# Queries and keys of all head pairs by Strassen's scheme ahead of attention, and the gates' token sums read back from DRAM, in a one-core hybrid trunk kernel

## The chip, the cores and the metric

The kernel runs on one core of a Trainium2 chip. The metric is the device time of one execution in microseconds (us), the median of several runs. The core has a matrix engine (TensorE, PE in the profile, with PEld for its weight loads), a vector engine (VectorE, DVE), an activation engine (ScalarE, ACT), a general engine (GpSimd, POOL), and SyncE (SP), which here only issues DMAs. PE writes its sums into PSUM banks (128 partitions by 512 float32), and DVE and ACT read them from there.

## The reference

One layer of a streaming encoder over 1024 tokens of width 1024, in float32. Cut to what matters:

```python
proj = x @ w_in
q_a, k_a, v_a, f_a, q_b, f_b, i_b, g_b, gate_a, gate_b = split(proj)
# branch A: forgetting attention, 8 heads of 64
F = cumsum(log_sigmoid(f_a + b_f))
y_a = softmax(where(causal, q_a @ k_a.T / 8 + F[t] - F[s], -inf)) @ v_a
# branch B: gated linear recurrence (HGRN2), 4 heads of 128
f = lb + (1 - lb) * sigmoid(f_b)
S_t = diag(f_t) S_{t-1} + (1 - f_t) v_t^T ;  o_t = S_t^T silu(q_b)_t
y_b = rmsnorm(o_b) * norm_g * sigmoid(g_b)
# merge, output projection, layer norm, SwiGLU, layer norm
merged = sigmoid(gate_a) * (y_a @ w_pa) + sigmoid(gate_b) * (y_b @ w_pb)
x = layer_norm(ALPHA * x + merged @ w_o)
x = layer_norm(ALPHA * x + (silu(g) * u) @ w_ff_out)     # u, g = split(x @ w_ff_in)
```

## The kernel before

**Products.** Every large float32 operand is split into a rounded high part and the rest (`split`: a cast on ACT, a subtraction on DVE), and a product is three matmuls, high by high, high by low and low by high (`mm3`, L449). x is held transposed and split in four tiles, `xh` and `xl`, in quarters A11, A12, A21, A22 (token half, and half of the channels).

**Strassen.** Most of the large products go by Strassen's scheme in Winograd's form: seven products p1 to p7 of blocks in place of eight. On the token side they need the quarters themselves (p1, p2, p4) and four sums of quarters: S1 for p5, S2 for p6, S3 for p7, S4 for p3 (`vops`, made for the values from L640 on). On the weight side they need block differences, made on DVE. Results are put together from p1, u2 = p1 + p6, u3 = u2 + p7 and so on. `skip_group_check` with `start=False` lets a product add onto what a bank holds already.

**Stages, in program order.** Values of both branches by Strassen (`vx`, `vy`: all eight banks); forget gates; queries and keys of head pair 0 by Strassen (`qk_first`, L720), while S1 stands in the place of A21, which is then restored from the raw quarter `a21`; attention for pairs 0 to 3 (`attention`, L763), with q and k of the next pair made directly after each (`qk_project`, L708: eight chunks by three matmuls for each of two weights and two token halves, PE's `qps` and `kps`); the recurrence's projections (`hgrn_project`, PE's `bps`) and heads (`hgrn`, L884); gates (`gate`: PE's `gps`; `gate_part`: `ge`; the rest in Strassen pairs, `gs`); branch projections (`pps`); output projection (`o`); layer norm; feed-forward by Strassen (`fa` to `fd`, then `p`); layer norm and output.

**Attention.** For a head, two rows of `box1` hold the broadcast sums of log f, plain and masked; DVE makes the masked row from the plain one and the constant `causal` (L770 to L773). For each block of 128 queries, scores go to a bank, DVE adds the row and takes the running minimum (`tensor_tensor_reduce`), ACT takes the exponential with its sum, DVE the reciprocal, POOL scales the block, PE transposes it, ACT and DVE split it, PE multiplies it with the values. `qk_heads` (L695) turns a bank with q or k of a pair into the tiles q2, k2, kl of its two heads, with the high part in one half of the partitions and the low part in the other.

**Gates.** The last twelve gate blocks go by Strassen. Their token sums S1 to S4 are made anew: x is loaded raw (`xr`, L1129) and `sums4` (L479) subtracts and splits on DVE and ACT.

**Order and storage.** Nothing is issued as it is written down. Each call is put in a list (`Plan.add`), with what it depends on. `Plan.schedule` (L170) places all calls with estimated durations, `improve` (L334) tries several ranks, and `issue` sends them in the best order found; so nearly every instruction of the profile has the line L363. An engine then works its calls strictly in that order. Tiles come from tags with a fixed number of buffers (`BUFS`, L378), handed out in order within a tag, PSUM banks likewise (`SPREAD`). `plan.early` lowers a call's rank, so that the gates' and projections' weights are drawn forward.

```python
    qk = qk_first()
    for p in range(4):
        attention(p, qk)
        if p < 3:
            qk = qk_project(p + 1)
        else:
            qfg = hgrn_project(0)
```

Of the kernel before, what the change touches and what calls it, by code (L numbers as in the profile page):

```python
# [16 lines left out]
P = 128  # L17
# [17 lines left out]
ROUNDS = 20  # L35
MARGIN = 1.06
SLACK = 400.0
SWITCH = 300.0
ALPHA = 2.0 ** 0.25
# [16 lines left out]

class Plan:
# [4 lines left out]
    OWN = {"PE": 0.0, "ACT": 0.0, "DVE": 127.0, "POOL": 60.0, "SP": 2500.0}  # L62
    SETS = {AF.Exp: 0, AF.Ln: 0, AF.Sigmoid: 1, AF.Silu: 2}

    def __init__(self, tc):
        self.tc = tc
        self.calls, self.tiles, self.log, self.first = [], {}, {}, {}
        self.queues, self.rank = {}, []
        self.early = 0
        self.loose = set()  # L70

# [22 lines left out]
    def add(self, q, method, args, kw):  # L94
# [7 lines left out]
        if method == "copy_predicated":  # L102
            ins.append(outs[0])
        n = len(self.calls)
        self.rank.append(n - self.early)
        pred = set()
# [21 lines left out]
        both = sum(str(v.space).endswith("SB") and v.free_size() > 128 for v in ins) > 1  # L128
        self.calls.append((q, method, args, kw, pred, names, fresh, self.cost(q.name, method, outs, ins, kw), both))

    def cost(self, eng, method, outs, ins, kw):
# [27 lines left out]
        if eng == "POOL":  # L159
            if method == "tensor_tensor" and kw.get("op") == ALU.pow:  # L160
# [9 lines left out]
    def schedule(self, slack, wait):  # L170
# [13 lines left out]
        dma_free = 0.0  # L184
        fifo, slots = {}, {}
# [15 lines left out]
        while done < len(calls):  # L201
            best = None
            for q, av in avail.items():
                for i in av:
# [16 lines left out]
                    if not ok:  # L221
                        continue
                    if q == "ACT":
# [14 lines left out]
            if q == "SP":  # L238
                start = max(t + 100, dma_free)
                dma_free = start + d  # L240
                free[q] = t + 60
                fin = dma_free
            else:
# [6 lines left out]
                fin = t + d  # L250
                free[q] = fin
# [35 lines left out]
    def lag(self, i, u, slack):  # L287
        q, uq = self.calls[i][0].name, self.calls[u][0].name
        lat = self.OWN[q] if uq == q else self.LAT[q]
# [4 lines left out]
    def latest(self, slack):  # L294
# [7 lines left out]
        for old, i in self.after:  # L302
            for m in by.get(old, ()):
                users[m].append((i, self.LAT[calls[m][0].name] + 60))
# [29 lines left out]
    def improve(self, slack, wait):  # L334
# [4 lines left out]
        for _ in range(ROUNDS):  # L339
            last, self.rank = self.turn, self.latest(slack)  # L340
# [26 lines left out]
def trunk(ctx: ExitStack, tc, a: dict, out: bass.AP):  # L367
# [30 lines left out]
    def small(shape, name, bufs=4):  # L398
        return plan.tile(cst, shape, F32, "c_" + name, name, bufs)
# [66 lines left out]


# [116 lines left out]
    def forget_gates():  # L584

        LO, NC = 32, KC + 4
        wfx = keep([P, NC, HA], "wfx", F32, "lnst")
# [49 lines left out]
    bf = const("bf", [NT * HA, 1])  # L637
# [14 lines left out]
    for c in range(4):  # L652
# [5 lines left out]
        split(vops["p7"][0][c], vops["p7"][1][c], s3)  # L658
        sync.dma_start(s3, a["xT"][c][:, hs(1)])
# [60 lines left out]
    def qk_first():  # L720

        g, u = (take("hl", [KC, P], f"w{n}0_r") for n in "qk")
        for b, t in enumerate((g, u)):
            sync.dma_start(t, a["w_qk"][b, 0])
        b11, b12, b21, b22 = g[:, :4], u[:, :4], g[:, 4:], u[:, 4:]
        t2 = take("ph", [4, P], "wqk_t2")
        p1, u2, p5 = (half("ph", f"qk0_{i}") for i in ("p1", "u2", "p5"))
        oa, ob, oc = (bank(t, f"qk0_{t}") for t in ("s", "pt", "s"))
        tiles = qk_tiles(0)

        def mul(p, src, o, first):
            T = [take(f"w{x}0" if p in ("p6", "p2", "p7") else "tt", [4, P], f"Tqk{p}{x}", F32R) for x in "hl"]
            split(*T, src)
            more = {} if first else {"skip_group_check": True}
            for c in range(4):
                mm3(o, T[0][:, c], T[1][:, c], vops[p][0][c], vops[p][1][c], first and c == 0, c == 3, more)

        dve.tensor_sub(b12, b12, b11)
        mul("p5", b12, oc, True)
        act.copy(p5, oc)  # L740
        split4(A21, a21)
        mul("p1", b11, oa, True)
        act.copy(p1, oa)
        mul("p2", b21, oa, False)
        dve.tensor_sub(t2, b22, b12)
        qk_heads(0, 0, oa, *tiles)
        mul("p6", t2, ob, True)
        dve.tensor_add(u2, ob, p1)
        mul("p3", b22, oc, False)
        dve.tensor_add(u2, oc, u2)  # L750
        qk_heads(1, 0, u2, *tiles)
        dve.tensor_sub(b11, t2, b11)
        mul("p7", b11, ob, False)
        dve.tensor_add(p5, p1, p5)
        dve.tensor_add(p5, ob, p5)
        qk_heads(1, 1, p5, *tiles)
        dve.tensor_sub(b21, b21, t2)
        mul("p4", b21, ob, False)
        dve.tensor_add(p1, ob, p1)
        qk_heads(0, 1, p1, *tiles)  # L760
        return tiles

    def attention(p, qk):  # L763
        q2, k2, kl = qk
        for i in range(2):
# [12 lines left out]
            for qb in range(NT):  # L778
                n = (qb + 1) * P
                pt = full("pf", f"p{h}_{qb}") if qb > 3 else half("ph", f"p{h}_{qb}")  # L780
                soft = small([P, 5], "soft")
# [973 lines left out]
```

## Time and profile before

| | us |
|---|---|
| median of 3 runs | 1446.02 (1444.09 to 1447.37) |
| span of the profiled execution | 1441.5 |
| PE busy in it | 1430.0 |
| DVE busy | 1112.8 |
| ACT busy | 668.6 |
| POOL busy | 87.2 |

The profile is of one execution. Its span runs from the first to the last instruction; the time of a run is measured around it. "Busy" of an engine is the time covered by its instructions; since matmuls overlap, PE's busy time and the mean duration of a matmul say less than the number of matmuls in a stretch of time. A group's row has the line, engine, operation, the written tile and the tiles read, the shapes, the count, then busy us and mean ns, then the engine's idle time just before these instructions and what ended it. A wait's row has us in total, times and the longest.

### The profile page before, as it was taken

To read this page: it belongs to the slowest core of one execution; us is meant where nothing else is said; L and a number is where in the kernel's file an instruction comes from. 1 tells how busy PE (TensorE), PEld (TensorE's weight loads), DVE (VectorE), ACT (ScalarE), POOL (GpSimd) and SP (SyncE) were. 2 spreads that over 40 slices of the span, in tenths; PEclk is the share of its full clock that TensorE was granted. 3 is DMA by queue.
4 is the path that set the end of the run, shared out by engine and by line. 5 is a ranking of instruction groups with operands and counts; after the bars stand their busy time and mean duration, and the time that the engine had idled before them with its cause. 6 is when DMAs were issued, how large, how long until landed. Compare 5 with 4: busy or idle time off the path is not lost.

```text
span 1441.5 us, 18901 instructions
## 1 busy us (share of the span) xinstructions
PE 1430.0 (99%) x6782; PEld 1188.2 (82%) x6782; DVE 1112.8 (77%) x1952; ACT 668.6 (46%) x1167; POOL 87.2 (6%) x100
## 2 busy tenths in 40 slices
PE   9999999999999999999999999999999999999997
PEld 7788888888888888788888888888888888888886
DVE  8998778567998999845857997666677776798596
ACT  5547768667767663344511443323333334434330
POOL 0002213120100110000000000000000000000011
PEclk9999999999999999999999999999999999999999
DMA  7022212211111455858500233233333326977632
GB/s 270 32 89 67 95 60 74 63 60 51 38 59 46 153 170 164 255 181 290 176 0 2 102 95 124 96 110 110 110 110 110 97 92 201 346 276 235 209 129 85
DMA packets 74029, 181.30 MB, mean 126 GB/s; under 512 B 8384, under 2 KB 9792, under 8 KB 73936
## 3 DMA queue, kind: packets, MB, share of 16 engines
q1 hardware_dynamic: 73936, 180.11, 37.9%
q8 instruction: 53, 0.87, 0.3%
q14 instruction: 40, 0.33, 0.1%
HBM read 139.90 MB, written 40.17 MB: 125 GB/s over the span
## 4 chain that ended last, share of the span: by engine, by line
PE 97%; DVE 2%; DMA 1%; issue 0%; ACT 0%; SPq 0%; DVEq 0%; ACTq 0%
PE p L363 14%; PE fb L363 12%; PE bps L363 9%; PE fc L363 8%; PE fa L363 8%; PE o L363 6%; PE pps L363 6%; PE gs L363 5%; PE vx L363 4%; PE gps L363 3%; PE s L363 2%; PE pv L363 2%; PE qps L363 2%; PE kps L363 2%; PE vy L363 2%; PE pt L363 2%
## 5 line engine op out<-in xcount | busy, mean ns | idle before, releaser
L363 PE MATMUL p<-dp 128*128 128x512 f32 (+1 forms) x957 | 210.1, 382 | 0.0
L363 PEld LDWEIGHTS p<-dp 128*128 128x128 f32 x957 | 175.1, 188 | 34.8
L363 PE MATMUL fc<-xs,Tp 128*128 128x512 f32 x528 | 127.3, 389 | 0.6 <-ACT Tp L363 0.6
L363 PE MATMUL fb<-xs,Tp 128*128 128x512 f32 x528 | 127.2, 389 | 0.0
L363 PEld LDWEIGHTS fc<-xs,Tp 128*128 128x128 f32 x528 | 99.1, 188 | 21.6 <-ACT Tp L363 1.0
L363 PEld LDWEIGHTS fb<-xs,Tp 128*128 128x128 f32 x528 | 99.1, 188 | 20.5
L363 PE MATMUL fa<-x,Tp 128*128 128x512 f32 x480 | 115.6, 389 | 0.0
L363 ACT CAST Tp<-t 128x512 fp32r<-128x512 f32 x88 | 54.2, 619 | 118.8 <-PE fc L363 64.8
L363 DVE TENSOR_TENSOR Tp<-t,Tp 128x512 fp32r<-128x512 f32 x88 | 60.6, 690 | 60.5 <-ACT Tp L363 59.9
L363 PEld LDWEIGHTS fa<-x,Tp 128*128 128x128 f32 x480 | 90.1, 188 | 18.7
L363 PE MATMUL bps<-xh,wb_h 128*128 128x512 f32 x192 | 76.2, 397 | 0.0
L363 PE MATMUL bps<-xl,wb_h 128*128 128x512 f32 x192 | 76.0, 396 | 0.0
L363 PE MATMUL bps<-xh,wb_l 128*128 128x512 f32 x192 | 75.5, 396 | 0.0
L363 POOL TENSOR_TENSOR norm<-norm,mhalf 128x1 f32<-128x1 f32 x16 | 17.2, 1075 | 886.3 <-DVE norm L363 886.3
L363 ACT CAST dp<-dap 128x1024 fp32r<-128x1024 f32 (+1 forms) x42 | 41.0, 979 | 57.8 <-PE p L363 35.7
L363 POOL TENSOR_SCALAR p<-p,soft 128x384 f32<-128x384 f32 (+4 forms) x64 | 51.9, 817 | 261.0 <-DVE soft L363 235.2
L363 DVE TENSOR_TENSOR tl<-pt,th 128x512 fp32r<-128x512 f32 (+1 forms) x96 | 52.2, 554 | 19.7 <-ACT th L363 15.5
L363 ACT CAST th<-pt 128x512 fp32r<-128x512 f32 (+1 forms) x96 | 45.5, 479 | 34.9 <-PE pt L363 30.8
L363 DVE TENSOR_TENSOR dp<-dap,dp 128x1024 fp32r<-128x1024 f32 (+1 forms) x42 | 47.4, 1132 | 15.9 <-ACT dp L363 15.7
L363 PE MATMUL fb<-x,Tp 128*128 128x512 f32 x240 | 57.7, 389 | 0.0
L363 PE MATMUL pt<-ident,p 128*128 128x128 f32 x288 | 53.8, 273 | 0.0
L363 ACT CAST Tp<-wg_r 128x512 fp32r<-128x512 f32 x40 | 24.9, 623 | 62.1 <-PE fb L363 30.2
(565 smaller groups left out, 3476.6 us busy)
## 6 DMA issues: line engine op xcount, KB each, us to landing
dbp<-in_w_fo SPq DMA_DIRECT2D x45, 512.0 KB, 5.3
dap<-a_d SPq DMA_DIRECT2D x35, 512.0 KB, 4.3
wg_r<-in_w_ff SPq DMA_DIRECT2D x22, 512.0 KB, 4.0
wu_r<-in_w_ff SPq DMA_DIRECT2D x22, 512.0 KB, 3.6
a_d<-ar SPq DMA_DIRECT2D x42, 256.0 KB, 2.7
a_d<-as SPq DMA_DIRECT2D x33, 256.0 KB, 3.4
wg_r<-in_w_g SPq DMA_DIRECT2D x16, 512.0 KB, 4.4
sg<-gate_d SPq DMA_DIRECT2D x32, 256.0 KB, 3.4
```

The costliest lines, as they stand in the source:

```text
L363: getattr(q.engine, method)(*args, **kw)
```

## The change

- `qk_project` goes. `qk_first` now runs `qk_strassen` for pairs 1, 2, 3 and 0 in that order, ahead of attention, with weights in the tags `hl` and `kb` by turns and two sets of three banks by turns. p6, p7 and p4 add onto the bank of p1; ACT copies the bank out in between (p1, u2, u3 in `p5`). Casts stay on ACT.
- Results of pairs 1 to 3 are stored to DRAM (`qk_d`, each head's rows twice, so that one load fills both halves of the partitions), and `qk_load` brings them back in the place of `qk_project` and makes q2, k2, kl from SBUF.
- The token sums S1 (already split) and S2 to S4 (single, not split) are stored in DRAM while they are made for the values; the gates load S1 into the place of A21 and split S2 to S4 on their return. The loads of raw x for the gates and `sums4`'s subtractions go.
- The masked row is a load of a full-width `causal` and an adding DMA (issued by POOL) of the broadcast row onto it.
- Reciprocals of row sums are taken for three blocks and then one, and POOL's scaling follows.
- In the recurrence, one scaling moves from DVE to ACT, and a subtraction goes into the bias of ACT's exponentials (two of 512 columns become eight of 128).
- Small constants share the tile `few`; `lnst` takes the tag `mask`.
- The planner has costs for DMAs issued by POOL (at most three in flight), 500 ns in place of 60 for an issue on SP, 300 in place of 358 bytes/ns for a transfer, and 24 ranks in place of 20, most with a random slack. Two sets of calls are held behind an earlier one (`plan.behind`): the load of attention's output behind the last token sum's split, and the first Silu of the feed-forward behind the first sums.

Its core:

```diff
-ROUNDS = 20
+ROUNDS = 24
+RING = 3
...
+    SOFT, LANDS, RATE = 950.0, 1050.0, 190.0
...
-        return float(o.nbytes()) / 358.0
+        return float(o.nbytes()) / 300.0
...
-                free[q] = t + 60
+                free[q] = t + 500
...
-            last, self.rank = self.turn, self.latest(slack)
+        vary = np.random.default_rng(1)
+        for n in range(ROUNDS):
+            last, self.rank = self.turn, self.latest(slack if n < 6 else slack * vary.uniform(0, 3))
...
+    s1_d = dram.tile([P, 2, 4, NB], F32, name="s1_d")
+    sum_d = dram.tile([3, 4, P, NB], F32, name="sum_d")
...
         split(vops["p6"][0][c], vops["p6"][1][c], a22[c])
         split(vops["p7"][0][c], vops["p7"][1][c], s3)
+        sync.dma_start(sum_d[0, c], a22[c])
+        sync.dma_start(sum_d[1, c], s3)
         sync.dma_start(s3, a["xT"][c][:, hs(1)])
...
-    causal = const("causal", [P, 2, P], BF16, "mask")
...
         split(vops["p3"][0][c], vops["p3"][1][c], a22[c])
+        sync.dma_start(sum_d[2, c], a22[c])
...
-    def qk_project(p):
-        tiles = qk_tiles(p)
-        for b in range(2):
-            plan.early = AHEAD
-            w = weights(a["w_qk"][b, p], [KC, P], f"w{'qk'[b]}{p}", 0)
-            plan.early = 0
-            for hf in range(2):
-                o = bank("g", f"{'qk'[b]}ps{p}_{hf}")
-                project(o, w, hf)
-                qk_heads(b, hf, o, *tiles)
-        return tiles
-
...
+    qk_d = dram.tile([4, 2, 2, 2, DH, S], F32, name="qk_d")
+    for n, x in enumerate((xh, xl)):
+        sync.dma_start(s1_d[:, n], f(x[0][:, :, hs(1)]))
+    lanes = [0]
+
+    def qk_strassen(p, wtags, btags, tiles=None):
+
+        g, u = (take(t, [KC, P], f"w{n}{p}_r") for t, n in zip(wtags, "qk"))
         for b, t in enumerate((g, u)):
+            sync.dma_start(t, a["w_qk"][b, p])
         b11, b12, b21, b22 = g[:, :4], u[:, :4], g[:, 4:], u[:, 4:]
+        p1, p5 = (half("ph", f"qk{p}_{i}") for i in ("p1", "p5"))
+        oa, ob, oc = (bank(t, f"qk{p}_{t}") for t in btags)
+
+        def mul(n, src, o, first):
+            lane = lanes[0]
+            lanes[0] ^= 1
+            T = [take(f"w{x}{lane}", [4, P], f"Tqk{p}{n}{x}", F32R) for x in "hl"]
             split(*T, src)
             more = {} if first else {"skip_group_check": True}
             for c in range(4):
+                mm3(o, T[0][:, c], T[1][:, c], vops[n][0][c], vops[n][1][c], first and c == 0, c == 3, more)
+
+        def put(b, hf, o):
+            if tiles:
+                return qk_heads(b, hf, o, *tiles())
+            if o is oa:
+                t = half("gt", f"qk{p}_o")
+                act.copy(t, o)
+                o = t
+            for i in range(2):
+                for j in range(2):
+                    sync.dma_start(qk_d[p, b, i, j, :, hs(hf)], o[i * DH:(i + 1) * DH])
+
+        mul("p1", b11, oa, True)
+        act.copy(p1, oa)
         dve.tensor_sub(b12, b12, b11)
         mul("p5", b12, oc, True)
+        if tiles:
+            split4(A21, a21)
+        t2 = take("tt", [4, P], f"wqk{p}_t2")
         dve.tensor_sub(t2, b22, b12)
+        mul("p2", b21, ob, True)
+        dve.tensor_add(p1, ob, p1)
+        put(0, 0, p1)
+        mul("p6", t2, oa, False)
+        u2 = half("tt", f"qk{p}_u2")
+        act.copy(u2, oa)
+        dve.tensor_sub(b11, t2, b11)
+        mul("p7", b11, oa, False)
+        act.copy(p5, oa)
+        dve.tensor_add(p5, oc, p5)
+        put(1, 1, p5)
         mul("p3", b22, oc, False)
         dve.tensor_add(u2, oc, u2)
+        put(1, 0, u2)
         dve.tensor_sub(b21, b21, t2)
+        mul("p4", b21, oa, False)
+        put(0, 1, oa)
+
...
+    def qk_load(p):
+        q2, k2, kl = qk_tiles(p)
+        for b in range(2):
+            for hf in range(2):
+                for i in range(2):
+                    ot = slice((1 - i) * DH, (2 - i) * DH)
+                    raw = half(f"w{'hl'[i]}0", f"qkr{p}_{b}{hf}{i}")
+                    sync.dma_start(raw, qk_d[p, b, i, :, :, hs(hf)].rearrange("j d t -> (j d) t"))
+                    if b == 0:
+                        act.activation(q2[i][:, hs(hf)], raw, AF.Copy, scale=-0.125)
+                        dve.scalar_tensor_tensor(q2[i][ot, hs(hf)], raw[ot], -0.125, f(q2[i])[ot, hs(hf)],
+                                                 op0=ALU.mult, op1=ALU.subtract)
+                    else:
+                        act.copy(k2[i][:, hs(hf)], raw)
+                        dve.tensor_sub(kl[i][:, hs(hf)], raw, f(k2[i])[:, hs(hf)])
+        return q2, k2, kl
+
+    def qk_first():
+        made = []
+
+        def tiles():
+            if not made:
+                made.extend(qk_tiles(0))
+            return made
+
+        for p, w, b in ((1, "hl", 0), (2, "kb", 1), (3, "hl", 0), (0, "kb", 1)):
+            qk_strassen(p, (w, w), (("s", "pt", "s"), ("h", "pv", "h"))[b], None if p else tiles)
+        return made
 
     def attention(p, qk):
         q2, k2, kl = qk
...
-            for hf in range(2):
-                plain, masked = (nfx[:, b0 + 4 * hf:b0 + 4 * hf + 4].rearrange("p (j c) t -> p j c t", c=2) for b0 in (0, NT))
-                dve.tensor_add(masked, plain, causal[:, None].to_broadcast([P, 2, 2, P]))
+            sync.dma_start(box1[:, r + 1, :], a["causal"])
+            pool.dma_start(box1[:, r + 1, :], nf_d[h].partition_broadcast(P), accum_op=ALU.add)
...
+                if qb % 4 == 0:
+                    sums = small([P, 8], "sums", 3, "ss")
+                sm, rs = sums[:, qb % 4:qb % 4 + 1], sums[:, 4 + qb % 4:5 + qb % 4]
...
-                dve.reciprocal(rs, sm)
-                pool.tensor_scalar(pt[:, :n], pt[:, :n], rs, 1.0, op0=ALU.mult, op1=ALU.mult)
                 pr.append(pt)
+                if qb % 4 > 1:
+                    lo = 0 if qb % 4 == 2 else 3
+                    dve.reciprocal(sums[:, 4 + lo:5 + qb % 4], sums[:, lo:1 + qb % 4])
+                    for j in range(qb - qb % 4 + lo, qb + 1):
+                        w, rs = (j + 1) * P, sums[:, 4 + j % 4:5 + j % 4]
+                        pool.tensor_scalar(pr[j][:, :w], pr[j][:, :w], rs, 1.0, op0=ALU.mult, op1=ALU.mult)
...
-        dve.tensor_scalar(fk, fk, olb[:, h:h + 1], lb[:, h:h + 1], op0=ALU.mult, op1=ALU.add)
+        act.activation(fk, fk, AF.Identity, scale=olb[:, h:h + 1], bias=lb[:, h:h + 1])
...
-            dve.tensor_sub(kd.rearrange("p (c j t) -> p c j t", c=2, t=P), bw,
-                           tot.rearrange("p j c -> p c j")[:, :, :, None].to_broadcast([P, 2, 4, P]))
-            act.activation(qeb[:, odd], kd[:, odd], AF.Exp, scale=-1.0)
-            act.activation(kd[:, even], kd[:, even], AF.Exp, scale=-1.0)
+            for j in range(4):
+                for c, t in enumerate((kd, qeb)):
+                    w = blk(4 * c + j)
+                    act.activation(t[:, w], b[:, w], AF.Exp, bias=tot[:, j, c:c + 1], scale=-1.0)
...
-            qk = qk_project(p + 1)
+            qk = qk_load(p + 1)
...
-    xr = []
-    for c in range(4):
-        two = [full(("wr0", "wr1")[j] if c == 0 else "qk", f"xg{c + 4 * j}_r") for j in range(2)]
-        for j in range(2):
-            sync.dma_start(two[j], a["xT"][c + 4 * j])
-        xr.append(two)
-    q11, q21, q12, q22 = ([x[j][:, hs(m)] for x in xr] for j, m in ((0, 0), (0, 1), (1, 0), (1, 1)))
+
+    def reload(m, tag, name):
+        t = take(tag, [2, 4, NB], name, F32R)
+        for c in range(0, 4, 2):
+            raw = take("qk", [2, NB], f"{name}_r{c}")
+            sync.dma_start(raw, sum_d[m, c:c + 2].rearrange("c p t -> p c t"))
+            for j in range(2):
+                split(t[:, 0, c + j], t[:, 1, c + j], raw[:, j])
+        return [[t[:, n, c, :] for c in range(4)] for n in range(2)]
 
...
-    gops["p5"] = operand1("x", "gs1")
-    sums4(gops["p5"], q22, q21, q22, False)
+    gops["p5"] = quarter(0, 1)
+    for n, x in enumerate((xh, xl)):
+        for j in range(2):
+            sync.dma_start(f(x[0][:, 2 * j:2 * j + 2, hs(1)]), s1_d[:, n, 2 * j:2 * j + 2])
...
-    gops["p6"] = operand1("m", "gs2")
-    sums4(gops["p6"], q22, q22, q11, True)
+    gops["p6"] = reload(0, "x", "gs2")
...
-    gops["p7"] = operand4(("pf",) * 4, "gs3")
-    sums4(gops["p7"], q11, q11, q21, True)
+    gops["p7"] = reload(1, "v", "gs3")
...
-    gops["p3"] = operand1("v", "gs4")
-    sums4(gops["p3"], q12, q12, q22, True)
+    gops["p3"] = reload(2, "m", "gs4")
+    loaded = len(plan.calls) - 1
...
+                plan.behind = (loaded,)
...
+        plan.behind = (summed,)
         act.activation(k.sl, o[0], AF.Silu)
+        plan.behind = ()
...
-    causal = np.stack([causal, causal.T], axis=1).astype(ml_dtypes.bfloat16)
+    causal = np.tile(np.concatenate([causal, causal.T], axis=1), (1, NT // 2))
```

More of the change, by code (lines that the diff above doesn't have):

```diff
@@ L69, in __init__ @@
         self.early = 0
+        self.lands = []
         self.loose = set()
+        self.behind = ()
     def queue(self, name, engine):
@@ L105, in add @@
         self.rank.append(n - self.early)
-        pred = set()
+        pred = set(self.behind)
         names = set()
@@ L128, in add @@
         both = sum(str(v.space).endswith("SB") and v.free_size() > 128 for v in ins) > 1
+        self.lands.append(self.LANDS + o_bytes(outs[0]) / self.RATE if q.name == "POOL" and method == "dma_start" else 0.0)
         self.calls.append((q, method, args, kw, pred, names, fresh, self.cost(q.name, method, outs, ins, kw), both))
@@ L222, in schedule @@
                         continue
+                    if self.lands[i]:
+                        t = max(t, ring[-RING])
                     if q == "ACT":
@@ L249, in schedule @@
                         d += 1283
-                fin = t + d
-                free[q] = fin
+                free[q] = t + d
+                fin = t + d + self.lands[i]
+                if self.lands[i]:
+                    fin = max(fin, ring[-1] + self.lands[i] - self.LANDS)
+                    ring.append(fin)
             self.times[i] = t
@@ L288, in lag @@
         q, uq = self.calls[i][0].name, self.calls[u][0].name
-        lat = self.OWN[q] if uq == q else self.LAT[q]
+        lat = self.lands[i] + (self.OWN[q] if uq == q else self.LAT[q])
         if uq == "PE" and q != "PE":
@@ L586, in forget_gates @@
         LO, NC = 32, KC + 4
-        wfx = keep([P, NC, HA], "wfx", F32, "lnst")
+        wfx = keep([P, NC, HA], "wfx", F32, "mask")
         sync.dma_start(wfx[:, :KC], a["w_f"])
@@ L635, in forget_sums @@
         sync.dma_start(nf_d.rearrange("h (t p) -> (h t) p", p=P), nf)
-    bf = const("bf", [NT * HA, 1])
+    few = keep([P, 28], "few")
+    bf, ng, warm, mhalf, lbl = few[:NT * HA, :1], few[:, 1:2], few[:, 2:3], few[:, 4:8], few[:, 8:12]
+    lbt = few[:, 12:28].rearrange("p (i h) -> p i h", h=HB)
+    sync.dma_start(bf, a["bf"])
     before = const("before", [NT * HA, NT * HA + 2], F32, "once")
@@ L836, in trunk @@
     lmask = const("lmask", [P, 2, MASKS], U16, "mask")
-    ng = const("ng", [P, 1])
-    lbl = const("lbl", [P, HB])
-    lbt = keep([P, 4, HB], "lbt")
+    sync.dma_start(ng, a["ng"])
+    sync.dma_start(lbl, a["lbl"])
     lbe, lbs, lb, olb = (lbt[:, i, :] for i in range(4))
-    mhalf = keep([P, 4], "mhalf")
     dve.memset(mhalf, -0.5)
@@ L1512, in trunk @@
         k.sl = half("gt", f"sl{k.c}")
+        plan.behind = (summed,)
         act.activation(k.sl, o[0], AF.Silu)
+        plan.behind = ()
     for k in ks:
```

54 lines of the change are left out of this document (14 added, 40 removed).

## The prediction

> **What bounds the kernel now.** I read the page's busy lines and chain of waits first, then the busy time by stage, then PE's own waits.
>
> ```profile
> span 1441.5 us, 18901 instructions
> PE 1430.0 (99%) x6782; PEld 1188.2 (82%) x6782; DVE 1112.8 (77%) x1952; ACT 668.6 (46%) x1167; POOL 87.2 (6%) x100
> ...
> PE 97%; DVE 2%; DMA 1%; issue 0%; ACT 0%; SPq 0%; DVEq 0%; ACTq 0%
> ```
>
> The chain is 97% TensorE. A busy PE need not be a full one, since matmuls overlap: the mean "duration" of a 128x512 matmul is 0.39 to 0.41 us (in the groups quoted below), but its place in the stream is shorter. Two views give it, the stages (us, then busy us and count of PE, PEld, DVE, ACT, POOL, the granted clock, DMA share, GB/s) and the chain in order of time (start, length):
>
> ```profile
> core 0: us, PE busy (x) PEld busy (x) DVE busy (x) ACT busy (x) POOL busy (x), PEclk, DMA share, GB/s
> ...
> 89.00:108.00 19.00, 19.00 (x86) 15.54 (x85) 16.88 (x32) 12.19 (x22) 0.00 (x0) 1.00 0.32 113
> 108.00:324.00 216.00, 215.98 (x1168) 181.66 (x1167) 158.15 (x486) 153.42 (x331) 51.88 (x64) 1.00 0.22 70
> 324.00:524.00 200.00, 200.00 (x1086) 171.95 (x1085) 173.82 (x280) 139.65 (x249) 14.24 (x15) 1.00 0.26 83
> 524.00:623.00 99.00, 97.83 (x442) 80.63 (x441) 82.96 (x130) 38.16 (x68) 3.71 (x2) 1.00 0.60 180
> ...
> 840.00:1223.00 383.00, 383.00 (x1690) 317.14 (x1691) 273.24 (x412) 124.26 (x204) 0.00 (x0) 1.00 0.37 116
> 1223.00:1442.00 219.00, 210.13 (x959) 174.99 (x957) 171.77 (x220) 73.01 (x81) 9.59 (x8) 0.99 0.61 214
> ```
> ```profile
> 16.65 10.88 PE vy L363 x48
> ...
> 592.83 6.06 DMA yr<-ya_d
> ```
>
> In the feed-forward stage 1690 matmuls take 383.00 us, so one is worth 0.2266 us; the chain's 48 in 10.88 us say 0.2267. That pitch, not 0.39, prices a matmul that goes or comes. The stages are: first pair's queries and keys (89 to 108), attention (108 to 324), gated recurrence (324 to 524), gates (524 to 623). In none of them does PE stand idle for long; all its waits are these (us, times, longest):
>
> ```profile
> PE vy L363 <- DVE mhalf L363: 1.2, 1, 1.2
> PE gs L363 <- DVE gu L363: 1.2, 2, 0.8
> PE fc L363 <- ACT Tp L363: 0.6, 1, 0.6
> ```
>
> So the kernel is one queue of matmuls. Fewer of them shorten it one for one, as long as every stage still has the next matmul ready; work taken from another engine is worth nothing by itself.
>
> **Matmuls removed.** Pairs 1 to 3 now make q and k directly: two weights, two halves, 8 chunks, 3 matmuls each = 96 a pair. The trace has them as six groups of 48, of which two:
>
> ```profile
> L363 PE MATMUL qps<-xl,wq_h 128*128 128x512 f32 x48 | 19.8, 412 | 0.0
> ...
> L363 PE MATMUL kps<-xl,wk_h 128*128 128x512 f32 x48 | 18.9, 393 | 0.0
> ```
>
> Strassen needs 7 products of 4 chunks by 3 = 84 a pair, as pair 0 already does. That is 12 fewer in each of three pairs: 36 x 0.2267 = **8.2 us less PE**. No other edit changes the number of matmuls.
>
> The Trainium skill (TensorE: Matmul & The Clock Gate, Back-to-back issue gap) gives a sustained 131 ns for 512 columns beside weight loads, and 216 ns for a lone one. An estimate by the first would make this gain 36 x 0.131 = 4.7 us, the time 3.5 us longer. The trace does not agree with it: 0.2267 us in both views, with a weight load for each matmul. I give that reading no chance.
>
> **The work that the three pairs bring ahead of attention.** A pair has 7 casts on ACT and 7 subtractions on DVE to split the blocks, 4 block sums and 3 corrections on DVE, 3 copies out of the bank on ACT. The nearest rows:
>
> ```profile
> L363 DVE TENSOR_TENSOR Tp<-wg_r,Tp 128x512 fp32r<-128x512 f32 x40 | 27.6, 691 | 0.2
> L363 ACT CAST Tp<-wg_r 128x512 fp32r<-128x512 f32 x40 | 24.9, 623 | 62.1 <-PE fb L363 30.2 <-issue 29.8 <-PE fc L363 2.1
> L363 ACT COPY p<-fa 128x512 f32<-128x512 f32 x20 | 11.8, 589 | 38.4 <-PE fa L363 38.4
> ```
>
> DVE: 14 x 0.69 = 9.7 us, ACT: 7 x 0.62 + 3 x 0.59 (and one more copy for the store) = 6.7 us, against 84 x 0.2267 = 19.0 us of PE. Half covered twice over: I cost it at nothing. It stops being nothing if a product waits for its bank; that is the second rival. Pair 0's stage had DVE at 16.88 of 19.00 us, with PE at 19.00. Each of the three pairs also issues 16 stores of 128 KB and later 8 loads; SP issues no more than some 24 in the pair's 19 us of PE, and a load or store lands in 2.5 to 4.1 us (the DMA rows below). Taken at nothing, with the first use much later; were each pair's load exposed at the head change, it would be 4.1 us three times. Weights come from DRAM in the shadow of the pair before.
>
> **Attention without its filler.** What leaves this stage, or shrinks in it:
>
> ```profile
> L363 DVE TENSOR_TENSOR box<-box,causal 128x512 f32<-128x512 f32 x15 | 10.1, 695 | 0.1
> L363 DVE RECIPROCAL soft<-soft 128x1 f32<-128x1 f32 x64 | 10.0, 158 | 4.8 <-ACT p L363 4.5
> L363 DVE SCALAR_TENSOR_TENSOR q<-qps,q 64x512 fp32r<-64x512 f32 x12 | 8.3, 688 | 2.5 <-ACT q L363 2.3
> L363 DVE TENSOR_TENSOR kl<-kps,k 64x512 fp32r<-64x512 f32 x12 | 8.2, 688 | 15.7 <-ACT k L363 15.6
> L363 DVE TENSOR_TENSOR wk_l<-wk_r,wk_h 128x512 fp32r<-128x512 f32 x6 | 4.7, 778 | 6.7 <-ACT wk_h L363 6.6
> L363 DVE TENSOR_TENSOR wq_l<-wq_r,wq_h 128x512 fp32r<-128x512 f32 x5 | 3.4, 689 | 0.7 <-ACT wq_h L363 0.6
> ...
> L363 ACT CAST k<-kps 64x512 fp32r<-64x512 f32 x24 | 13.9, 581 | 8.9 <-PE kps L363 7.8 <-DVE kl L363 0.8
> L363 ACT CAST kl<-kl 64x512 fp32r<-64x512 f32 x16 | 9.9, 619 | 2.2 <-DVE kl L363 2.0
> L363 ACT ACTIVATE q<-qps 64x512 fp32r<-64x512 f32 x12 | 7.1, 593 | 3.8 <-DVE q L363 2.2 <-PE qps L363 1.3
> ```
>
> PE loses some 280 matmuls of q and k that lie in this window: 216 - 63.5 = 152.5 us stay. DVE loses the mask additions (10.1), half of the 64 reciprocals (5.0, since they are taken for one or three blocks at a time) and the weight splits (8.1); its 24 operations on q and k stay, from loaded copies: 158.2 - 23.2 = 135 us. ACT's 13.9 + 12 of 16 of 9.9 + 7.1 become 24 casts of 0.62, and the weight casts (about 6) go: some 133 us. So DVE and ACT would stand at 88% of a stage that needs only 152 us of PE, where they stood at 73 and 71%. The recurrence stage shows what is possible: DVE 173.82 of 200 us (87%) with PE full. There two edits move to ACT:
>
> ```profile
> L363 DVE TENSOR_TENSOR kd<-hbb,tot 128x1024 f32<-128x1024 f32 x4 | 4.9, 1216 | 0.0
> L363 DVE TENSOR_SCALAR hbf<-hbf,lbt 128x1024 f32<-128x1024 f32 x4 | 3.2, 809 | 2.3 <-ACT hbf L363 2.3
> ```
>
> which leaves DVE 165.7 us. Over both stages DVE needs 301 us beside 352 of PE, 85.5%. The matmuls of later gates and of the recurrence's projections can be drawn forward as filler, and the order is made by a planner over the whole kernel. Cost: from 0 (DVE may run at 87%) to 24 us (if it manages no more than the 80% which the two stages together have now, (158.2 + 173.8) / 416: 301 / 0.8 = 376). I take 1 us, nearest to the recurrence's row, for the change from the projections to the first head.
>
> **Masks, the POOL queue, DMA.**
>
> ```profile
> box<-nf_d SPq DMA_DIRECT2D x8, 512.0 KB, 4.1
> ...
> gate_d<-gt SPq DMA_DIRECT2D x10, 256.0 KB, 2.5
> ...
> SPq L363 <- DVE soft L363: 23.4, 8, 9.4
> ```
>
> The masked row is now a load of the mask and an adding DMA from POOL's queue. No adding DMA is in the trace: between one plain landing (4.1 us) and two and a half (10 us, if the sum halves its rate), after the mask's own 4.1. A head takes 152 / 8 = 19 us and the rows are double, so it fits; exposed in every head it would be 8 x 4.1 = 33 us. Behind it in POOL's queue stand the scalings of the probabilities (64, 51.88 us in 216), for which transposes on PE wait; behind SP's wait for the freed row (now 23.4 us in 8 times, harmless) stand q and k loads. Zero taken. The sums' stores ahead (5 MB in all) and the reads later go where the DMAs are 0.2 to 0.6 busy.
>
> **Gates.** 16 subtractions and one operand's four splits leave a stage in which DVE is at 82.96 of 99 us:
>
> ```profile
> L363 DVE TENSOR_TENSOR xg_r<-xg_r 128x512 f32<-128x512 f32 x16 | 10.7, 683 | 0.7 <-DMA xg_r<-in_xT 0.7
> ...
> 584.18 0.39 PE L363 MATMUL gs<-gs,Tgp_10l 128*128 128x512 f32 x1
> ...
> 585.38 0.47 PE L363 MATMUL gs<-gs3h,Tgp_10h 128*128 128x512 f32 x1 [0.81 <-DVE gu L363]
> ```
>
> DVE falls by 10.7 + 2.8 = 13.5 us. Here PE waited for a late DVE sum: 585.38 - 584.18 - 0.23 = 0.97 us, and a second time some 0.5 us. I count both as regained: **1.5 us**. Next in line is the load of attention's output, the 6.06 us DMA of the chain, which the diff holds back until the last sum has been asked for; it may be late by up to those 6.06, or not at all; zero taken, since 85 us of PE work stand between.
>
> **The rest** (planner constants, one more seed of orders, packed small tiles, Silu held behind the first sums): the feed-forward's 383 us have no gap to win. At best the 0.6 us of the ACT wait goes; at worst a new order opens as much. Zero.
>
> **Sum.** Against the profiled execution: 1441.5 - 8.2 (matmuls) - 1.5 (gates) + 1.0 (first head) = 1432.8 us of span. The runs have a median of 1446.02 (1444.09 to 1447.37), 4.5 above that span; I leave those 4.5 as they are: **1437.3 us**. Its own range: 1433 (no cost at the first head, the 0.6 and some 2 us more found by the new order) to 1441 (no gain at the gates, 3 us of small waits).
>
> **Rival 1: attention starves PE (slower).** With 63.5 us of filler gone, DVE and ACT set the stage's pace. It decides from the point where DVE's share over attention and recurrence can't pass 301 / (352 + 8.2) = 83.5%; below that the 8.2 are lost. At 82% it is 367 - 352 = 15 us: 1446.0 - 8.2 + 15 = 1453, at 80% 1462. For it: the softmax is a serial chain over DVE, ACT, POOL and PE, and DVE was never above 73% in it. Against it: 87% in the recurrence, and filler that can come early. 17%, mostly at the cheap end near 1450.
>
> A rule speaks for this rival: the Trainium skill (SBUF — State Buffer, Who interferes with whom) says that a VectorE instruction with two SBUF inputs and a GpSimd instruction that reads SBUF shut each other out for its whole length. The trace agrees: wk_l, split beside POOL's scalings, took 778 ns, the same operation in the feed-forward 691. The 24 operations on q and k now have both inputs in SBUF instead of one in PSUM: by the rule an estimated 24 x 0.09 = 2 us more DVE.
>
> **Rival 2: chained banks.** In each pair three products (p6, p7, p4) add onto a bank that ACT must first have copied. Left bare, one costs what the late sum cost above, 0.97 us: 4 pairs x 3 = 11.7 us, giving 1449.5; half bare 1443.7. It decides where the other pair's products are not ready in between. Against it: two sets of three banks, and pair 0's similar chain ran at 19.00 of 19.00 us. 11%.
>
> **Chances.** Forecast 72%, rival 1 17%, rival 2 11%. About 0.2%, 2.9 us, is what a measurement of this kernel can tell from no change (1443.1 to 1448.9). Faster: 72 + 2 + 4 = 78%; same 4 + 4 = 8%; slower 11 + 3 = 14%. Range 1432.5 to 1448.5: it takes in rival 2 half bare and the cheap end of rival 1, and leaves out some 17%.
>
> **What would show it.** 36 fewer matmuls for q and k, at 0.2267 us each; the 336 of all four pairs between 89 and 165 us, with no PE wait on ACT copies (else rival 2); attention then some 150 us long, DVE near 88% in it, PE full (else rival 1: idle PE ahead of the scores, transposes or pv, ended by DVE, ACT or POOL); no wait of PE for gu; the feed-forward again at 0.2266. I am wrong if any stage's matmuls take more than their pitch by over 5 us in sum, or if PE waits for the loaded q, k or masks.

## The result, and the profile after

The changed kernel takes 1435.30 us (median of 4 runs, 1432.97 to 1435.98) against 1445.05 us (4 runs, 1443.66 to 1447.37): a ratio of 0.9928, 95% interval 0.9913 to 0.9943, some 10 us. The page's first lines, and the end of the chain of waits:

```profile
span 1432.9 us, 19015 instructions
...
PE 1421.4 (99%) x6746; PEld 1182.0 (82%) x6746; DVE 1101.2 (77%) x1904; ACT 669.3 (47%) x1187; POOL 92.0 (6%) x108
...
PE 96%; DVE 3%; DMA 1%; ACT 0%; issue 0%; SPq 0%; DVEq 0%; ACTq 0%
```

6782 - 6746 = 36 matmuls fewer. The stages of the changed kernel (columns as before): all four pairs' queries and keys, attention, recurrence, gates, feed-forward.

```profile
89.00:165.00 76.00, 76.00 (x337) 62.69 (x336) 42.29 (x72) 31.12 (x57) 1.06 (x1) 1.00 0.62 165
165.00:328.00 163.00, 162.01 (x927) 137.11 (x926) 140.87 (x433) 134.30 (x302) 58.42 (x71) 1.00 0.51 156
328.00:524.00 196.00, 195.92 (x1067) 167.98 (x1066) 167.67 (x272) 143.93 (x271) 15.40 (x15) 1.00 0.25 82
524.00:616.00 92.00, 92.00 (x419) 76.48 (x418) 70.51 (x109) 34.24 (x60) 1.59 (x2) 1.00 0.65 197
...
840.00:1223.00 383.00, 383.00 (x1692) 317.13 (x1691) 272.29 (x407) 125.70 (x205) 0.00 (x0) 1.00 0.38 122
```

The Strassen stage is dense, 337 matmuls in 76.00 us. Attention, 216 us before, is 163 us long with DVE at 86% and ACT at 82%; it is the only stage from 89 us to the gates' end in which PE visibly idles. PE's waits, all of them:

```profile
PE vy L381 <- DVE few L381: 1.2, 1, 1.2
PE vx L381 <- ACT xh L381: 1.1, 1, 1.1
PE pv L381 <- ACT th L381: 0.8, 1, 0.8
PE fc L381 <- ACT Tp L381: 0.8, 1, 0.8
PE pt L381 <- DVE tl L381: 0.2, 1, 0.2
```

The two waits on `gu` are gone; pv and pt are new. The timeline shows what they are:

```profile
271.35 0.62 ACT L381 CAST k<-qkr 128x512 fp32r<-128x512 f32 x1 [2.29 <-DMA qkr<-qk_d]
271.88 0.47 ACT L381 CAST th<-pt 128x384 fp32r<-128x384 f32 x1
...
272.40 0.44 PE L381 MATMUL pv<-th,vhl 128*128 128x384 f32 x1 [0.84 <-ACT th L381]
```

ACT stands 2.29 us at the cast of a loaded k, whose DMA is late. Behind it in ACT's order is the cast `th` that PE's next product reads. A wait that concerns only the next pair thus reaches PE through the queue of ACT. The loads and the adding DMA land so (median us last):

```profile
qkr<-qk_d SPq DMA_DIRECT2D x24, 256.0 KB, 4.7
...
box<-nf_d POOLq DMA_DIRECT2D x8, 512.0 KB, 6.8
```

The adding DMA's 6.8 us lie between the 4.1 and the 10 us that I had allowed for, and no wait of PE is at a mask.

### The profile page after: what moved, and what is told of

Read it like the earlier page. It is cut to its first block, busy times and chain, and to the rows that moved or that the text cites. A ratio compares the mean times of both kernels' runs of the same rounds, so it can differ in the third digit from the quotient of the medians.

```text
span 1432.9 us, 19015 instructions
## 1 busy us (share of the span) xinstructions
PE 1421.4 (99%) x6746; PEld 1182.0 (82%) x6746; DVE 1101.2 (77%) x1904; ACT 669.3 (47%) x1187; POOL 92.0 (6%) x108
## 4 chain that ended last, share of the span: by engine, by line
PE 96%; DVE 3%; DMA 1%; ACT 0%; issue 0%; SPq 0%; DVEq 0%; ACTq 0%
PE p L381 15%; PE fb L381 11%; PE bps L381 9%; PE fc L381 8%; PE fa L381 8%; PE gs L381 6%; PE o L381 6%; PE pps L381 6%; PE vx L381 4%; PE gps L381 3%; PE qk_s L381 2%; PE vy L381 2%; PE qk_h L381 2%; PE s L381 2%; PE pv L381 2%; PE pt L381 2%
## 5 line engine op out<-in xcount | busy, mean ns | idle before, releaser
L381 POOL TENSOR_TENSOR norm<-norm,few 128x1 f32<-128x1 f32 x16 | 15.4, 962 | 880.9 <-DVE norm L381 880.9
L381 POOL TENSOR_SCALAR p<-p,sums 128x128 f32<-128x128 f32 (+3 forms) x64 | 52.6, 853 | 88.2 <-DVE sums L381 61.8
L381 ACT ACTIVATE p<-p,soft 128x640 f32<-128x640 f32 (+5 forms) x64 | 49.9, 780 | 6.4 <-DVE soft L381 6.1
L381 PEld LDWEIGHTS fb<-x,Tp 128*128 128x128 f32 x240 | 45.0, 188 | 9.4
```

Source lines behind the costliest of these rows:

```text
L381: getattr(q.engine, method)(*args, **kw)
```

## Experiments

Ratios are to the kernel before, run on the same chip; 0.001 is 1.4 us. All kernels start from the changed one, unless said otherwise. The planner makes a new order for each.

**Queries and keys directly again** (e1_direct), all else as changed:

```diff
-        for p, w, b in ((1, "hl", 0), (2, "kb", 1), (3, "hl", 0), (0, "kb", 1)):
+        for p, w, b in ((0, "hl", 0),):
...
-            qk = qk_load(p + 1)
+            qk = qk_project(p + 1)
```

> The changed kernel with pairs 1 to 3 made directly again between the heads (288 matmuls in place of 252), all else as changed. My theory (36 matmuls at 0.2267 us each are the gain): 8.2 us above the changed kernel, so a ratio to the kernel before of 0.9928 + 8.2/1445 = 0.9985 (0.9970 to 1.0000). Rival (the gain comes from the other edits, the new order of the planner above all): at most 3 us above the changed kernel, a ratio under 0.995.

Measured: 1441.29 us, 0.9979 (0.9970 to 0.9988). That is 0.0051, 7.4 us, above the changed kernel. The two spans, 1439.5 and 1432.9, differ by 6.6: the 8.2 us of matmuls less the new waits. My theory's range holds it, the rival's does not.

**Gates' sums made anew** (e2_gates): raw x loaded, `sums4`, nothing of the sums in DRAM; `p5`, `p7` and `p3` are treated as `p6` is here.

```diff
-        sync.dma_start(sum_d[0, c], a22[c])
-        sync.dma_start(sum_d[1, c], s3)
...
-    gops["p6"] = reload(0, "x", "gs2")
+    gops["p6"] = operand1("m", "gs2")
+    sums4(gops["p6"], q22, q22, q11, True)
```

> The changed kernel with the gates' token sums made anew from raw x (no sums in DRAM, 16 subtractions and four splits back on DVE). My theory: DVE is late again for the gates' sums and PE waits for it some 1.5 us: ratio 0.9928 + 0.0010 = 0.9938 (0.993 to 0.995), with a PE wait on DVE between 520 and 620 us. Rival (the new order alone took these waits away): no such wait, ratio 0.9928 within 0.0005.

Measured: 1441.60 us, 0.9978 (0.9968 to 0.9988): 7 us over the changed kernel, not 1.5, and no faster than e1_direct although it has 36 matmuls fewer. Its gates and PE's longest waits:

```profile
524.00:624.00 100.00, 97.11 (x435) 79.07 (x435) 85.64 (x137) 39.03 (x76) 3.83 (x2) 1.00 0.59 181
```
```profile
PE pv L381 <- ACT th L381: 1.7, 1, 1.7
PE gs L381 <- ACT gp L381: 1.2, 1, 1.2
...
PE gs L381 <- DVE gu L381: 0.9, 1, 0.9
...
PE op L381 <- DVE ob L381: 0.5, 1, 0.5
```

PE idles 2.9 us in 524 to 624 us, where the changed kernel's gates have no idle PE. Then there is the wait at a loaded k again, 1.7 us, and what follows it in the clock (last section). The profiled execution is the slowest of the eight (1443.51; the fastest took 1439.75). Some 1.6 us of its excess lie at the start, where the edit does not explain them: from 4 to 10 us it runs 15 matmuls, the changed kernel's profiled execution 22.

**Another order of the same work**: the planner's seed 2 in place of 1, in the changed kernel (e8_seed2) and in e2_gates (e2_seed2).

```diff
-        vary = np.random.default_rng(1)
+        vary = np.random.default_rng(2)
```

> The changed kernel with another seed for the planner's random slack: the same instructions in another order. It measures what an order by itself is worth. Theory (small waits come and go by chance of the order): between 0 and 5 us more than the changed kernel, ratio 0.992 to 0.9965. Rival (the order found is settled by the work): ratio 0.9928 within 0.0007.

> The kernel with the gates' sums made anew, with the same other seed. If the 7 us which that edit cost are the work's (DVE late for the sums at the end of the recurrence and in the gates), they come again: 4 to 8 us over e8_seed2, with PE waits between 500 and 600 us. If they were the luck of one order, the two seeds differ by more than that: 0 to 3 us over e8_seed2.

Measured: 1435.69 us, 0.9939 (0.9925 to 0.9954), and 1438.99 us, 0.9970 (0.9957 to 0.9983). The first can't be told from the changed kernel, though its waits are others (none at a loaded k, one of 1.5 us on `gu`). The second is 0.0031, 4.5 us, above it, with waits on `gu` (2.5 us in 3), `gp` (1.0) and at a loaded k (1.7) once more; the profiled execution is again the slowest, of six. So the gates' edit is worth some 4 to 7 us beside Strassen, in both orders.

**The planner alone**, in the kernel before (e6_planner): the `Plan` class of the changed kernel, 24 ranks. Of the diff to the kernel before:

```diff
-ROUNDS = 20
+ROUNDS = 24
...
-        for _ in range(ROUNDS):
-            last, self.rank = self.turn, self.latest(slack)
+        vary = np.random.default_rng(1)
+        for n in range(ROUNDS):
+            last, self.rank = self.turn, self.latest(slack if n < 6 else slack * vary.uniform(0, 3))
```

> The kernel before with the changed planner alone (its costs, 24 ranks, random slack); same work on every engine. My theory: nothing to win, since PE idles 3 us in all: ratio 1.000 (0.999 to 1.001). Rival (a better order is a good part of the gain): 0.997 or less.

Measured: 1441.74 us, 0.9982 (0.9973 to 0.9991): 2.6 us faster, between the two theories. All of PE's waits in it:

```profile
PE vy L381 <- DVE mhalf L381: 1.2, 1, 1.2
PE fc L381 <- ACT Tp L381: 0.8, 1, 0.8
PE vx L381 <- ACT xh L381: 0.3, 1, 0.3
```

The waits on `gu` are gone with the gates' sums still made on DVE. A new order alone removed what I had put down to DVE's relief. Those waits are 1.2 of the 2.2 us by which the two spans differ (1441.5 and 1439.3). Another 0.8 us lie behind the last matmul: 8.3 us follow it in the kernel before, 7.6 here and 7.4 in the changed kernel. Its end, in the kernel before, the changed kernel and e9_land4 (below):

```profile
1431.83 1.29 PE L363 MATMUL p<-dp 128*128 128x512 f32 x5
...
1424.27 1.24 PE L381 MATMUL p<-dp 128*128 128x256 f32 x9
...
1424.17 1.07 PE L381 MATMUL p<-dp 128*128 128x512 f32 x4
```

All these kernels have the same matmuls there; the new order puts 256 columns last in place of 512, so that DVE's addition and statistics behind them take 0.42 and 0.43 us in place of 0.68 and 0.69.

**Both undone** (e11_direct_gates): q and k direct, sums anew; its edit is that of e1_direct and that of e2_gates together.

> The changed kernel with both undone: pairs 1 to 3 made directly between the heads, and the gates' sums made anew from x. The fourth of four (direct or Strassen, sums anew or from DRAM), all other edits as changed. My new theory (the gates' edit is worth something only where Strassen has pressed attention and recurrence together): as the direct kernel with sums from DRAM, 0.9979 within 0.001. Rival (the gates' edit is worth its 3 to 7 us by itself, 13.5 us of DVE): 1.000 to 1.003, with PE waits on DVE in the gates.

Measured: 1445.42 us, 0.9999 (0.9990 to 1.0008). My number is missed; the rival's number is met within the interval, but not its mechanism: there is no PE wait in the gates (100.00 of 100.00 us busy from 524 on). In the profiled execution one wait of 2.2 us at the first head did it (`PE s <- DVE soft`), with the slow clock after it. Behind it stands a DMA: DVE is idle 3.1 us for `box` from `nf_d`, the first head's row, issued from 104 us on into DMA engines that are 0.95 to 1.06 busy until 116 us. In sum, 4.6 us are lost from 80 to 120 us where e1_direct loses 0.6, taken as matmuls started later than their pitch. Whether another order of the same work would stand at e1_direct was not tried. The four cells:

| | sums anew | sums from DRAM |
|---|---|---|
| direct | 0.9999 (no gates wait) | 0.9979 |
| Strassen | 0.9978, other seed 0.9970 | 0.9928, other seed 0.9939 |

By the times the gates' edit is worth 0.0020 (2.9 us) with direct q and k, and 0.0050 or 0.0031 with Strassen; Strassen is worth 0.0021 without that edit and 0.0051 with it. That the one needs the other is therefore likely, and the waits speak for it, but with one order for each direct kernel, and an order that by itself was worth 2.6 us (e6_planner), it is not shown.

**Masks and reciprocals back on DVE** (e5b_masks_recip): the code of the kernel before in these two places.

```diff
-            sync.dma_start(box1[:, r + 1, :], a["causal"])
-            pool.dma_start(box1[:, r + 1, :], nf_d[h].partition_broadcast(P), accum_op=ALU.add)
+            for hf in range(2):
...
+                dve.tensor_add(masked, plain, causal[:, None].to_broadcast([P, 2, 2, P]))
...
+                dve.reciprocal(rs, sm)
+                pool.tensor_scalar(pt[:, :n], pt[:, :n], rs, 1.0, op0=ALU.mult, op1=ALU.mult)
```

> The changed kernel with the masked rows made by DVE again and 64 single reciprocals: DVE has 10.8 + 5 us more in attention, 156 us where PE needs 163 (96%), and no adding DMA is left. My theory in the form of rival 1's ceiling: if DVE can't pass some 87% over attention and recurrence, these two stages grow from 359 to (156 + 168) / 0.87 = 372 us: 13 us more, ratio 1.002. If filler and order keep PE fed up to 90%, nothing: 0.993, and DVE had more room than I gave it. The other rival, that the adding DMA itself costs PE time (its landing late for a head), would show as a ratio under 0.9928.

Measured: 1436.74 us, 0.9945 (0.9933 to 0.9958), 2.5 us above the changed kernel, not 13. Attention in it:

```profile
165.00:330.00 165.00, 163.48 (x936) 139.02 (x935) 152.59 (x479) 135.51 (x307) 58.87 (x64) 1.00 0.36 115
```

DVE runs at 92% and PE still loses only 1.5 us. A ceiling near 87% does not exist here. No wait at a loaded k appears; with the mask's DMAs gone the DMA share is 0.36 in place of 0.51, which fits loads that were late for want of room, but one order doesn't show it.

**No filler in attention** (e4_nofill): every call of `gate` and `gate_part` held behind attention's last call.

```diff
+    plan.behind = (held,)
     for n in range(PLAIN):
         gate(n, 1)
...
+    plan.behind = ()
```

> The changed kernel with all plain and partial gates (288 matmuls, 65 us) held behind the last call of attention, so that attention has no filler but the recurrence's first projection. My theory (attention is DVE's and ACT's pace, 140 and 134 us of work, and PE is full only because gates fill it): PE's own work there is about 100 us, the stage takes 150 us or more, and the time grows by 35 to 50 us, to about 1475, with PE idle inside attention. Rival (the planner finds other work, or attention shrinks to its PE work): under 10 us.

Measured: 1473.6 us in one run, some 38 us more, as expected. Attention and PE's waits there:

```profile
165.00:330.00 165.00, 148.00 (x782) 109.74 (x781) 139.66 (x437) 132.51 (x296) 60.30 (x73) 0.99 0.45 133
```
```profile
PE pt L381 <- DVE tl L381: 8.4, 18, 1.3
PE s L381 <- DVE soft L381: 3.1, 6, 1.0
PE pv L381 <- ACT ya L381: 1.8, 4, 0.8
```

The stage isn't shorter although 145 matmuls left it. Its length is that of the softmax chain; PE fills it only with other work.

**A little less filler, fewer matmuls** (e7_plain2: `PLAIN = 2`, so 12 matmuls less in all and 72 less to fill with), **loads planned to land later** (e9_land4: the planner's landing 4.0 us for 2.5), and both (e10_land4_plain2).

```diff
-PLAIN = 4
+PLAIN = 2
```
```diff
-    LAT = {"PE": 197.0, "ACT": 131.0, "DVE": 128.0, "POOL": 66.0, "SP": 2500.0}
-    OWN = {"PE": 0.0, "ACT": 0.0, "DVE": 127.0, "POOL": 60.0, "SP": 2500.0}
+    LAT = {"PE": 197.0, "ACT": 131.0, "DVE": 128.0, "POOL": 66.0, "SP": 4000.0}
+    OWN = {"PE": 0.0, "ACT": 0.0, "DVE": 127.0, "POOL": 60.0, "SP": 4000.0}
```

> The changed kernel with two gate blocks instead of four made directly and two more by Strassen: 12 matmuls less in all (2.7 us), but 72 less of filler in attention and recurrence (16 us), where DVE would need 308 us beside 343 of PE (90%). If PE stays fed, ratio 0.9928 - 0.0019 = 0.991. If 90% is over what order and chains allow, the 16 us of lost filler show as PE waits on DVE or ACT in attention: ratio 0.993 or more.

> The changed kernel with the planner told that a DMA's landing takes 4.0 us in place of 2.5 (the profile has 4.7 us for the loads of q and k): the same work, loads issued earlier. Theory (the wait of 1.4 us in attention is ACT standing at a load of k that lands late): no PE wait on th with ACT idle for qkr ahead of it, up to 1.5 us less than the changed kernel, ratio 0.9918 to 0.993. Rival (the loads are late because the mask's DMAs fill the queues, whatever their issue time): the wait stays, ratio 0.993 or more.

> Both of the last two: 12 matmuls less and landings planned at 4.0 us. If both theories hold, 2.7 + up to 1.5 us less than the changed kernel: ratio 0.990 to 0.991. If filler is short, above 0.993 as the one with the two blocks alone.

Measured: 1443.69 us, 0.9994 (0.9985 to 1.0002); 1437.00 us, 0.9948 (0.9936 to 0.9961); 1444.08 us, 0.9997 (0.9988 to 1.0006). None beats the changed kernel. With 16 us less of filler, attention of e7_plain2 has PE busy 150.13 of 157 us and the waits of e4_nofill come back:

```profile
165.00:322.00 157.00, 150.13 (x845) 122.68 (x845) 136.07 (x428) 129.94 (x296) 61.13 (x71) 0.99 0.52 155
```
```profile
PE pv L381 <- ACT th L381: 2.8, 2, 2.0
PE pt L381 <- DVE tl L381: 1.6, 5, 0.7
PE s L381 <- DVE soft L381: 1.2, 4, 0.6
```

The longest of them, 2.0 us, is ACT at a loaded q again; but e10_land4_plain2 has no such wait of PE, is no faster, and has PE's other waits (`pt` 2.7 us in 6, `s` 1.7 in 3, `pv` 1.5 in 3). So the changed kernel stands close to the edge that rival 1 named. In e9_land4 PE has no wait at a loaded k left, as my theory had it (ACT still stands there, 2.9 us in 3), but the time is no better. Its last matmul ends at 1425.2 us, 0.3 us before that of the changed kernel; yet 9.2 us follow it in place of 7.4, because its order ends with 512 columns again (the third line shown under the planner), with DVE's work on another block in between. What this order won in attention it lost behind the last matmul, and the same 9.2 us stand in e10_land4_plain2.

**One set of banks** (e3_oneset): all pairs on the same three banks.

```diff
-            qk_strassen(p, (w, w), (("s", "pt", "s"), ("h", "pv", "h"))[b], None if p else tiles)
+            qk_strassen(p, (w, w), ("s", "pt", "s"), None if p else tiles)
```

> The changed kernel with all four pairs on one set of three banks (s, pt, s), so that no product of the next pair can stand between the chained ones until the bank of the pair before is copied out. My theory (rival 2's price is hidden by the other pair's products): some of the 12 copies come bare, one or two a pair at 0.97 us or less: 4 to 8 us above the changed kernel, ratio 0.9955 to 0.9985, with PE waits on ACT or DVE between 89 and 175 us. Rival (products of the same pair are enough cover, the second set is not needed): ratio 0.993 and no such wait. All bare would be 11.7 us, ratio 1.001.

Measured: 1438.45 us, 0.9958 (0.9944 to 0.9972), in my range, but not by my mechanism: PE has no wait between 89 and 165 us. Products of the same pair cover the copies, and rival 2 would not have come even without the second set. The profiled execution took 1434.39 us, the fastest of the five (to 1440.22); what the others lost is not in a trace and stays open.

## Why the prediction came out as it did

**Right, and shown:** the matmuls. 36 fewer at 0.2267 us, 8.2 us; e1_direct gives 7.4 us back by the ratio and 6.6 by the spans. The pitch, not the 0.39 us of the records, was the price. The Strassen stage ran full, and rival 2 was rightly small, with more cover than I counted.

**The first head's 1 us: right size by luck, wrong place.** The changed kernel loses about 1.4 us in attention at 271 us (PE idle 0.84 and 0.15 us, and two starts at less than pitch), at the load of a later pair's k, which I had taken "at nothing, with the first use much later". The bound that I gave for it, 4.1 us a head change, holds. What I missed was the queue: ACT's wait for a load that nobody needs yet holds the cast that PE needs now. By the sign that I had named myself, PE waiting for the loaded q and k, this term was wrong, if by little.

**Attention's work:** 135 us of DVE predicted, 140.9 measured. Of the 5.9 us, 2.6 are operations with two SBUF inputs beside POOL; another 2.7 are splits of `we`, gate weights drawn forward with the filler:

```profile
L381 DVE TENSOR_TENSOR kl<-qkr,k 128x512 fp32r<-128x512 f32 x12 | 10.4, 868 | 0.0
...
L381 DVE SCALAR_TENSOR_TENSOR q<-qkr,q 64x512 fp32r<-64x512 f32 x12 | 8.7, 722 | 0.2
...
L381 DVE TENSOR_TENSOR we_l<-we_r,we_h 128x512 fp32r<-128x512 f32 x4 | 2.7, 679 | 0.0
```

868 and 722 ns, where the direct form with one input in PSUM had 688 each: 2.6 us in 24 operations. These are means of two kinds: 17 of the 24 took 652 to 691 ns, and the other seven 848 to 1277 ns, each of them while a scaling ran on POOL. The rule on the port shared by VectorE and GpSimd, in the Trainium skill (SBUF — State Buffer, Who interferes with whom), agrees with it; the estimate drawn from it was 2 us. The 778 ns of `wk_l`, from which that estimate came, were such a mean too: one operation of 1217 ns beside a scaling, and five of 681 to 693 ns with none.

**Rival 1's ceiling was wrong, its filler right.** I took DVE's share as what decides (83.5% over two stages, 87% at best). DVE went to 92% in e5b_masks_recip for 1.5 us of PE. What decides is matmuls from elsewhere: 72 fewer cost the gain (e7_plain2), none left cost 38 us (e4_nofill).

**Gates and planner: the sum right, the terms not.** I gave the gates' edit 1.5 us, by DVE's relief, and the planner zero. The planner alone is worth 2.6 us and takes those very waits, and 0.8 us behind the last matmul besides. The gates' edit is worth 4 to 7 us beside Strassen, where PE waits in the gates without it (e2_gates, e2_seed2); with direct q and k no gates wait is there to be taken (e6_planner, e11_direct_gates). I added the two as if each were worth the same with and without the other. Without the gates' edit 3 to 4 of the 8.2 us are left by the four cells, and the rest goes into new waits.

**The 2 us between 1437.3 and 1435.3** come from comparing one profiled execution with a median of runs. I carried over 4.5 us, the median less the profiled span. In the changed kernel's profiled run only 1434.72 - 1432.9 = 1.8 us lie outside the span, and in every later run of the kernel before 1.9 or 2.0. So some 2.5 of the 4.5 us were an execution faster than the median. The changed kernel's median is only 2.4 us over its profiled span; this difference of 2.1 us, less 0.1 by which the span came out longer, is the miss. The span itself, 1432.8 predicted and 1432.9 measured, agrees by luck: up to the end of the last matmul the gain is 1433.1 - 1425.5 = 7.6 us, 1.1 less than the 8.7 of the sum, and 0.9 us behind it, for which the sum had no term, make up for most of that.

## What to carry to other kernels

Price a matmul by its pitch in a dense stretch, and a saving by what its cover loses: work moved ahead was also the filler of the stage it left. When one engine sets the pace, test edits in pairs, because one edit may be what keeps another's gain, and test each pair in more than one order, because an order alone was worth 2.6 us here. An engine that takes its work in order can pass on a wait for a load: a load needed later should not stand ahead of a cast that is needed now.

## What the runs showed of the hardware

One PE wait of about 2 us can cost nearly twice its length. In the profiled execution of e5b_masks_recip PE idles 1.92 us ahead of 594.66 us; the granted clock of the stretches that follow (third figure from the right, ahead of DMA share and GB/s) is then this:

```profile
592.00:594.00 2.00, 0.74 (x4) 0.28 (x2) 1.73 (x4) 1.57 (x2) 0.00 (x0) 1.00 0.23 68
...
596.00:598.00 2.00, 2.00 (x7) 1.52 (x6) 2.00 (x4) 0.29 (x1) 0.00 (x0) 0.51 0.93 289
598.00:600.00 2.00, 2.00 (x8) 1.60 (x7) 1.68 (x4) 0.62 (x1) 0.00 (x0) 0.64 0.93 263
600.00:602.00 2.00, 2.00 (x10) 1.67 (x9) 1.46 (x3) 0.00 (x0) 0.00 (x0) 1.00 0.55 210
```

The clock is halved for some 3.4 us, in which a 128x512 matmul takes 0.43 us in place of 0.23: about 1.7 us more. The same follows the waits at a loaded k in e2_gates and e2_seed2 (1.7 us each), the longest wait of e7_plain2 (2.0) and the wait at the first head in e11_direct_gates (2.2); in e4_nofill it comes at 181 us amid three waits of 0.7 to 1.1 us within 4 us. It does not follow the changed kernel's 1.4 us or e8_seed2's wait of 1.5. The Trainium skill (TensorE: Matmul & The Clock Gate, HAM oscillation — how this bites in real kernels) has such a drop for idle gaps over some 3.4 us; here 1.7 to 2.2 us were enough.

Each of these is one execution. The other four runs of e5b_masks_recip, with the same order, took 1436.02 to 1436.96 us where the profiled one took 1439.16, and their mean granted clock was 0.998 or 0.999 in place of 0.997. This fits a wait without the drop behind it in those four, but no trace of those four shows it; so the medians of the experiments may hold the drop or not. A single wait of 1.5 us stayed cheap in the traces, and one a little longer did not, which helps to make orders that look alike, and executions of one order, differ by 2 to 3 us.
